# Products within chunks of two heads, and rates of two directions, issued in turn on the two halves of TensorE's rows

## The chip, the cores and the metric

One program runs on one core of a Trainium2 chip. The metric is the device time of one execution in microseconds (us); the median of several executions stands for a kernel.

## What is computed

Two transformer layers of one kind, then one of another kind, on 512 tokens of width 1024, everything in fp32. The change lies in the third layer, in a recurrent branch that the reference writes as a scan over tokens, for 16 heads of 64 and two directions:

```python
def rwkv_prepare(z, shift_w, w0, w_up, a0, a_up, k_k, k_a):
    ...
    w_log = -jax.nn.softplus(-(w0[:, None, None, :] + jnp.einsum('btr,drc->dbtc', jnp.tanh(wd), w_up))) - 0.5
    decay = jnp.exp(-jnp.exp(w_log.astype(jnp.float32)))
    a = jax.nn.sigmoid(a0[:, None, None, :] + jnp.einsum('btr,drc->dbtc', ad, a_up))
    kk = head_l2norm(k * k_k)
    k_eff = k[None] * (1 + (a - 1) * k_a)
    ...

def wkv_scan(s0, scan_in):
    def step(s, inp):
        w, kk, a, k, v, r = inp
        sa = jnp.einsum('dbhij,dbhj->dbhi', s, kk)
        s = s * w[..., None, :] - sa[..., :, None] * (kk * a)[..., None, :] + v[..., :, None] * k[..., None, :]
        return s, jnp.einsum('dbhij,dbhj->dbhi', s, r)
    return lax.scan(step, s0, scan_in)
```

The rates are `a`, from `ad` (64 channels) and `a_up` of each direction. The scan runs over 256 context tokens and then 512 tokens.

## The kernel before, in words

The scan is done in chunks of 64 tokens. Two heads lie side by side on the 128 partitions (0 to 63 and 64 to 127), so there are 8 blocks of channels (`ct`), and each is cut into 3 groups of 4 chunks for each direction (`j` = 0, 1, 2; `j` = 0 is the context): 24 groups in all. A group goes through four pieces of work, each a Python generator:

- `decays` makes the decays and the rates of the group and from them the scaled operands `BK` and `KR`. The rates are two matmuls, one for each direction `d`, of `par[64:128, 2 + d]` with `AD[64:128]`, a contraction over 64 partitions, both on the upper half of TensorE's rows, into the two halves of one PSUM bank.
- `products` multiplies `BK` with `KR` within the chunks, for each direction and each of the two heads `h`: four matmuls contract over the 64 partitions of the head (`H[h]`), write 128 partitions of one bank, and VectorE masks that bank into `G` (line 1702). Then four transposes give `KB`. For `j` = 0 the moving operand has 64 columns, otherwise 128.
- `newton` inverts the triangular parts of `G` of both directions, in 18 steps of fp16 matmuls of 64 x 64 (tile `n`), with ScalarE and VectorE between them.
- `chain` carries the state through the group's 4 chunks, in 13 steps: `X` from state and `VS` (tile `c`), copied to `Xs`, times `U`, copied to `VS` (line 1792), times `KB` to the new state. At its end, for `j` > 0, 16 matmuls of 64 x 64 in fp32 make `O` from `G` and `VS`, and two adds (line 1817) take `O` out of its bank.

The order on each engine is the order of the code (`Pinned`). `weave` runs one slot for each group, of `TT` = 36 ticks: in slot s the chain of group s, the inversions of group s + 1, decays and products of group s + 2, and 48 steps of `fill`, matmuls of 128 rows (tile `mm`) that prepare later blocks. Each piece has a first tick, a last tick and a number of steps that are spread evenly: with `P0` = 17 the six steps of `products` come in ticks 17, 20, 23, 26, 29 and 32; the chain's last step, which makes `O`, comes in tick 27. An fp32 matmul stands in the trace as two weight loads and two matmuls. `xt()` hands out the two banks of tag `x` in turn; rates, products, transposes and `O` all take theirs from it.

Of the kernel before, what the change touches and what calls it, by code (L numbers as in the profile page):

```python
# [10 lines left out]
F32 = mybir.dt.float32  # L11
# [10 lines left out]
T = 512  # L22
NT = T // P
KD = D // P
RWT = 36, 30, 16, 17, 30, 48, 30
FR, SR = 8, 300
FR0 = 2.5, 4
FR1 = 1, 13
# [180 lines left out]
class Net:  # L209
# [1291 lines left out]
    def rwkv(self, hxh, hxl, hch, hcl, mmt2, bank2, lead):  # L1501
# [11 lines left out]
        with ExitStack() as st:  # L1513
# [54 lines left out]
            def block(ct, o):  # L1568

                cs = slice(ct * P, (ct + 1) * P)  # L1570
                o["cs"], o["ct"] = cs, ct
                par = o["par"] = pp.tile([P, 4, P], F32, tag="par", name=self.uid("par"), bufs=2)
                for d in range(2):
                    nc.sync.dma_start(par[0:64, d], a["rw_w_up_2"][0, d, :, cs])
                    nc.sync.dma_start(par[64:65, d], a["rw_w0_2"][0, d:d + 1, cs])
                    nc.sync.dma_start(par[64:128, 2 + d], a["rw_a_up_2"][0, d, :, cs])
                k = o["k"] = tl([P, TA], "k", 2)
                yield from proj(8 + ct, k)

                kks = tl([P, TA], "kks")  # L1580
                nc.vector.tensor_scalar(kks, k, self.kk_[:, ct:ct + 1], None, op0=ALU.mult)
                sq = tl([P, TA], "sq")
                nc.scalar.activation(sq, kks, AF.Square)
                r = o["r"] = tl([P, T], "r", 2)
                yield from proj(ct, r, False)
                ps = xt()
                for t in range(NM):
                    pe.matmul(ps[:, 2 * t:2 * t + 2], sq[:, t * P:(t + 1) * P], c["heads"], start=True, stop=True)
                rn = self.small.tile([P, 2 * NM], F32, tag="rn", name=self.uid("rn"))
                self.rstd(rn, ps[:, :2 * NM], 1.0, 1e-12)  # L1590
                rb = tl([P, TA], "sq").rearrange("p (t h i) -> p t h i", h=2, i=64)
                nc.vector.tensor_copy(rb, rn.rearrange("p (t h) -> p t h", h=2)[:, :, :, None].to_broadcast([P, NM, 2, 64]))
                v = tl([P, TA], "v")
                yield from proj(16 + ct, v)
                kkn = o["kkn"] = tl([P, TA], "kkn", 2)
                for s in rng:
                    ps = xt()
                    n = s.stop - s.start
                    for t in range(n // P):
                        pe.transpose(ps[:, t * P:(t + 1) * P], rb[:, s.start // P + t].rearrange("p h i -> p (h i)"), c["ident"])  # L1600
                    nc.vector.scalar_tensor_tensor(kkn[:, s], ps[:, :n], -0.5, kks[:, s], op0=ALU.mult, op1=ALU.mult)
                    yield
                o["v"] = v
# [27 lines left out]
            def decays(o, g):  # L1631

                ct, j, par = o["ct"], g["j"], o["par"]
                E, Em, ta, ke = tl([P, 2, 4, 65], "E"), tl([P, 2, 4, 64], "Em"), tl([P, 2, C], "ta"), tl([P, 2, C], "ke")
                WC = g["WC"] = tl([P, 2, 4], "WC", 3)
                tok = [slice(P * m0, P * m0 + C) for m0 in pairs(j)]
                ps = xt()
                for d in range(2):
                    for t in range(2):
                        n = tok[d].start + t * P  # L1640
                        pe.matmul(ps[:, (2 * d + t) * P:(2 * d + t + 1) * P], WD[:, n:n + P], par[:65, d], start=True, stop=True)
                th = tl([P, T], "th")
                nc.scalar.activation(th, ps, AF.Tanh, scale=0.5)
                nc.vector.tensor_scalar(th, th, 1.0, None, op0=ALU.add)
                yield
                ps = xt()
                for d in range(2):
                    pe.matmul(ps[:, C * d:C * d + C], par[64:128, 2 + d], AD[64:128, tok[d]], start=True, stop=True)
                for d in range(2):
                    nc.scalar.activation(ta[:, d], ps[:, C * d:C * d + C], AF.Tanh, scale=0.5, bias=self.a0h[:, KD * d + ct:KD * d + ct + 1])  # L1650
                nc.scalar.activation(ke, ta, AF.Identity, scale=self.kah[:, ct:ct + 1], bias=self.kab[:, ct:ct + 1])
                yield
                yield
                ps = xt()
                for d in range(2):
                    for t in range(2):
                        n = (2 * d + t) * P
                        pe.matmul(ps[:, n:n + P], th[:, n:n + P], c["chunk_" + "fb"[d]], start=True, stop=True)
                for d in range(2):
                    o1 = 1 - d  # L1660
                    nc.gpsimd.memset(E[:, d, :, 64 * d:64 * d + 1], 1.0)
                    nc.scalar.activation(E[:, d, :, o1:o1 + 64], ch(ps[:, C * d:C * d + C]), AF.Exp, scale=-K)
                    nc.vector.tensor_copy(WC[:, d], E[:, d, :, 64 * o1])
                nc.scalar.activation(Em.rearrange("p d c s -> p (d c s)"), ps, AF.Exp, scale=K)
                yield

                BK = g["BK"] = tl([P, 2, 2, 4, 64], "BK")
                KR = g["KR"] = tl([P, 2, 2, 4, 64], "KR", 3)
                pr = lambda x: x.rearrange("p (m e) s -> p m e s", e=2)
                for d in range(2):  # L1670
                    o1 = 1 - d
                    nc.gpsimd.tensor_tensor(ke[:, d], ke[:, d], o["k"][:, tok[d]], op=ALU.mult)
                    nc.vector.scalar_tensor_tensor(ta[:, d], ta[:, d], 1.0, o["kkn"][:, tok[d]], op0=ALU.add, op1=ALU.mult)
                    nc.vector.scalar_tensor_tensor(KR[:, d, :, 1:3], pr(ch(o["kkn"][:, tok[d]])), -2.0, pr(E[:, d, :, d:d + 64]), op0=ALU.mult, op1=ALU.mult)
                    if j:
                        xc = slice(tok[d].start - C, tok[d].stop - C)
                        nc.gpsimd.tensor_tensor(KR[:, d, :, 0:4:3], pr(ch(o["r"][:, xc])), pr(E[:, d, :, o1:o1 + 64]), op=ALU.mult)
                    nc.vector.tensor_tensor(BK[:, d, :, 1:3], pr(ch(ta[:, d])), pr(Em[:, d]), op=ALU.mult)
                    nc.vector.tensor_tensor(BK[:, d, :, 0:4:3], pr(ch(ke[:, d])), pr(Em[:, d]), op=ALU.mult)
                    yield  # L1680

            def products(o, g):
# [5 lines left out]
                for d in range(2):  # L1688
                    G = tl([P, 2, 4, P], "G", 5)
                    g["G"].append(G)  # L1690
                    for h in range(2):
                        rows = H[h]
                        ps = xt()
                        for i in range(4):
                            e = i % 2
                            if j:
                                pe.matmul(ps[:, P * i:P * i + P], bk2(rows, d, i),
                                          KR[rows, d, i // 2, 2 * e:2 * e + 2].rearrange("p a s -> p (a s)"), start=True, stop=True)
                            else:
                                off = P * i + 64 * (1 - e)  # L1700
                                pe.matmul(ps[:, off:off + 64], bk2(rows, d, i), KR[rows, d, i // 2, 1 + e], start=True, stop=True)
                        nc.vector.tensor_tensor(G[:, h].rearrange("p (m e) n -> p m (e n)", e=2)[:, :, kc],
                                                ps.rearrange("p (m n) -> p m n", m=2)[:, :, kc],
                                                c["mask_" + "fb"[d]][:, None, kc].to_broadcast([P, 2, kc.stop - kc.start]), op=ALU.mult)
                        yield

                    KB = tl([P, 2, 2, P], "KB", 5)
                    g["KB"].append(KB)
# [111 lines left out]
            def first():  # L1820
                z = tl([P, TA], "v")
                yield from proj(24, z)
                nc.scalar.activation(WD[0:64], z[0:64], AF.Tanh)
                nc.vector.tensor_copy(AD[64:128], z[64:128])
                z = tl([P, TA], "sq")[:, :T]
                yield from proj(25, z, False)
                nc.scalar.activation(SG, z, AF.Tanh, scale=0.5)
                nc.vector.tensor_scalar(SG, SG, 0.5, 0.5, op0=ALU.mult, op1=ALU.add)
# [97 lines left out]
            for s in range(-2, NG_):  # L1926
# [7 lines left out]
                if 0 <= s + 2 < NG_:  # L1934
                    if s > -2:
                        work.append((decays(os_[(s + 2) // 3], gs[s + 2]), 0, DE, 6))
                    work.append((products(os_[(s + 2) // 3], gs[s + 2]), P0, TT, 6))
                if s >= 3 and s % 3 == 0:
                    work.append((self.rwkv_post(os_[s // 3 - 1], tl, xt, SG, pp, pe), 0, TT, 4))
                if s % 3 == 1 and s + 2 < NG_:  # L1940
# [713 lines left out]
```

## Time and profile before

| | us |
|---|---|
| median of 3 runs | 4516.03 (4514.3 to 4528.95) |
| the profiled execution, its own time | 4530.77 |
| its span, first to last instruction | 4529.0 |
| stage of the slots | about 2000 to 3030 |

In the profile PE is TensorE's matmuls, PEld its weight loads, DVE VectorE, ACT ScalarE, POOL GpSimd. Matmuls are pipelined and their ends are modelled, so what a burst of them costs is read from its start to the start of what follows it on the same engine.

### The profile page before, as it was taken

What the parts mean: (1) busy time and instruction counts of PE and PEld (TensorE: products, weight loads), DVE (VectorE), ACT (ScalarE), POOL (GpSimd) and SP (SyncE); (2) the same over time, 40 slices, a digit from 0 to 9 for tenths busy, and PEclk for the clock granted to TensorE, in tenths of its full rate; (3) what the DMA queues carried; (4) which work ended last, traced back from release to release, by engine and by line L of the source; (5) the groups of instructions that cost most, each with busy time, mean ns of one, the idle gap of its engine ahead of it and who ended that gap; (6) DMA issues with size and microseconds to landing.
All of it is one profiled execution on the core that took longest, in us unless ns stands there. A gap on an engine that the chain in (4) does not pass through costs nothing. (4 is left out here: it accounts for less than half of the span.)

```text
span 4529.0 us, 83380 instructions
## 1 busy us (share of the span) xinstructions
PE 4225.4 (93%) x32239; PEld 3671.5 (81%) x32239; DVE 3076.7 (68%) x5903; ACT 1976.1 (44%) x4240; POOL 1698.9 (38%) x1501
## 2 busy tenths in 40 slices
PE   8999999899999899889999999998967889999998
PEld 6889988788888788777777777776866779999997
DVE  4665224656565656555666666645999797999999
ACT  3554234445332545444544455533334444444443
POOL 3324444333443534222333333314465102445443
PEclk8999999899999999989999899999989999999999
DMA  4325334333555422100000001156237557999997
GB/s 136 80 72 148 95 98 125 84 80 112 160 188 183 126 56 59 44 27 22 25 26 26 25 27 35 47 165 215 90 117 223 190 163 260 341 341 343 333 339 261
DMA packets 436982, 620.88 MB, mean 137 GB/s; under 512 B 32852, under 2 KB 318692, under 8 KB 436456
## 3 DMA queue, kind: packets, MB, share of 16 engines
q1 hardware_dynamic: 393384, 471.97, 33.3%
q0 software_dynamic: 36864, 134.23, 8.3%
q10 hardware_dynamic: 6336, 9.35, 0.7%
q8 instruction: 253, 4.15, 0.4%
q14 instruction: 145, 1.19, 0.1%
HBM read 549.36 MB, written 48.24 MB: 132 GB/s over the span
## 5 line engine op out<-in xcount | busy, mean ns | idle before, releaser
L62 POOL TENSOR_TENSOR wlo<-wraw,whi 128x512 fp32r<-128x512 f32 x451 | 613.1, 1365 | 887.9 <-ACT whi L62 849.1
L62 ACT CAST whi<-wraw 128x512 fp32r<-128x512 f32 x572 | 347.5, 617 | 556.3 <-PE mm L62 360.2
L62 PE MATMUL acc<-v,ah 128*128 128x512 f32 x1536 | 419.7, 396 | 4.3 <-ACT ah L62 4.3
L62 PE MATMUL u<-hph,u 128*128 128x384 f32 x1504 | 398.8, 336 | 0.0
L62 PE MATMUL mm<-whi,u 128*128 128x256 f32 x2048 | 377.8, 285 | 4.1 <-ACT u L62 2.4
L1497 POOL TENSOR_TENSOR wbl<-wblk,wbh 128x256 fp32r<-128x256 f32 (+1 forms) x184 | 149.9, 815 | 568.3 <-ACT wbh L1496 363.6
L62 PE MATMUL mm<-xh,whi 128*128 128x512 f32 (+2 forms) x880 | 342.7, 389 | 8.1 <-ACT r L62 5.1
L62 PEld LDWEIGHTS acc<-v,ah 128*128 128x128 f32 x1536 | 292.5, 191 | 60.3 <-ACT ah L62 4.6
L62 PE MATMUL mm<-xl,whi 128*128 128x512 f32 (+2 forms) x880 | 329.1, 374 | 0.0
L62 PEld LDWEIGHTS mm<-whi,u 128*128 128x128 f32 x2048 | 323.9, 194 | 6.1 <-ACT u L62 3.0
L62 PE MATMUL mm<-xh,wlo 128*128 128x512 f32 (+2 forms) x880 | 328.9, 374 | 0.0
L62 PE MATMUL mm<-wlo,u 128*128 128x256 f32 x1024 | 291.8, 285 | 4.9 <-POOL wlo L62 4.6
L62 PEld LDWEIGHTS u<-hph,u 128*128 128x128 f32 x1504 | 273.1, 188 | 3.7
L62 PE MATMUL acc<-v,al 128*128 128x512 f32 x768 | 243.8, 399 | 25.9 <-DVE al L62 25.9
L2555 POOL DMA_INDIRECT gr<-in_peer_u_dram,ei x128 | 165.0, 1289 | 251.7 <-DVE act L2569 158.3
L62 PE MATMUL u<-hpl,u 128*128 128x384 f32 x752 | 252.7, 336 | 0.0
L2555 POOL DMA_INDIRECT gr<-in_peer_v_dram,ei x128 | 170.0, 1328 | 183.4 <-DVE pr L2576 152.8
L62 PE MATMUL mm<-whi,xh 128*128 128x256 f32 x768 | 237.2, 309 | 0.0
L62 PE MATMUL mm<-whi,xl 128*128 128x256 f32 x768 | 220.8, 287 | 1.0 <-POOL xl L62 1.0
L62 PE MATMUL mm<-wlo,xh 128*128 128x256 f32 x768 | 220.3, 287 | 0.0
L62 PEld LDWEIGHTS mm<-wlo,u 128*128 128x128 f32 x1024 | 198.2, 194 | 6.2 <-POOL wlo L62 5.4
L62 DVE TENSOR_TENSOR wlo<-wraw,whi 128x512 fp32r<-128x512 f32 x121 | 102.5, 847 | 147.8 <-ACT whi L62 141.8
(598 smaller groups left out, 11876.2 us busy)
## 6 DMA issues: line engine op xcount, KB each, us to landing
raw<-in_ut_dram SPq DMA_DIRECT2D x128, 512.0 KB
raw<-in_peer_v_dram SPq DMA_DIRECT2D x128, 512.0 KB
wraw<-in_w_in_dram SPq DMA_DIRECT2D x184, 256.0 KB
wraw<-in_w_down_dram SPq DMA_DIRECT2D x160, 256.0 KB
wraw<-in_w_up_dram SPq DMA_DIRECT2D x152, 256.0 KB
mraw<-in_w_mod_dram SPq DMA_DIRECT2D x96, 256.0 KB
wg<-stage SPq DMA_DIRECT2D x12, 2048.0 KB
W<-wg SPq DMA_DIRECT2D x32, 768.0 KB
```

The source lines that it names most:

```text
L62: return lambda *a, **k: self.tc.keep_in_program_order(f(*a, **k))
L1497: (nc.vector if self.wn > WN and n % 2 else nc.gpsimd).tensor_tensor(lo, raw, hi.bitcast(F32), op=ALU.subtract)
L2555: tc.keep_in_program_order(nc.gpsimd.indirect_dma_start(out=r, out_offset=None, in_=w, in_offset=bass.IndirectOffsetOnAxis(ap=ei[:, i:i + ...
```

## The change

The four products of one head are no longer issued in one step and those of the other in the next. Both heads get a bank each at once, and the matmuls go head 0, head 1, head 0, head 1, and so on; both masks follow, and one yield. `products` then has four steps, which with `P0` = 20 come in ticks 20, 24, 28 and 32. The rates get one half of the rows for each direction, and a bank each: `par` and `AD` hold them on both halves, for which one DMA copies 64 x 768 values of `AD` once.

```diff
-RWT = 36, 30, 16, 17, 30, 48, 30
+RWT = 36, 30, 16, 20, 30, 48, 30
...
-                par = o["par"] = pp.tile([P, 4, P], F32, tag="par", name=self.uid("par"), bufs=2)
+                par = o["par"] = pp.tile([P, 3, P], F32, tag="par", name=self.uid("par"), bufs=2)
...
-                    nc.sync.dma_start(par[64:128, 2 + d], a["rw_a_up_2"][0, d, :, cs])
+                    nc.sync.dma_start(par[H[d], 2], a["rw_a_up_2"][0, d, :, cs])
...
-                ps = xt()
+                pss = [xt()[:, :C], xt()[:, :C]]
                 for d in range(2):
-                    pe.matmul(ps[:, C * d:C * d + C], par[64:128, 2 + d], AD[64:128, tok[d]], start=True, stop=True)
+                    pe.matmul(pss[d], par[H[d], 2], AD[H[d], tok[d]], start=True, stop=True)
                 for d in range(2):
-                    nc.scalar.activation(ta[:, d], ps[:, C * d:C * d + C], AF.Tanh, scale=0.5, bias=self.a0h[:, KD * d + ct:KD * d + ct + 1])
+                    nc.scalar.activation(ta[:, d], pss[d], AF.Tanh, scale=0.5, bias=self.a0h[:, KD * d + ct:KD * d + ct + 1])
...
-                    for h in range(2):
-                        rows = H[h]
-                        ps = xt()
-                        for i in range(4):
-                            e = i % 2
+
+                    pss = [xt(), xt()]
+                    for i in range(4):
+                        e = i % 2
+                        for rows, ps in zip(H, pss):
                             if j:
                                 pe.matmul(ps[:, P * i:P * i + P], bk2(rows, d, i),
                                           KR[rows, d, i // 2, 2 * e:2 * e + 2].rearrange("p a s -> p (a s)"), start=True, stop=True)
                             else:
                                 off = P * i + 64 * (1 - e)
                                 pe.matmul(ps[:, off:off + 64], bk2(rows, d, i), KR[rows, d, i // 2, 1 + e], start=True, stop=True)
+                    for h, ps in enumerate(pss):
                         nc.vector.tensor_tensor(G[:, h].rearrange("p (m e) n -> p m (e n)", e=2)[:, :, kc],
...
-                        yield
+                    yield
...
+                nc.sync.dma_start(AD[0:64], z[64:128])
...
-                    work.append((products(os_[(s + 2) // 3], gs[s + 2]), P0, TT, 6))
+                    work.append((products(os_[(s + 2) // 3], gs[s + 2]), P0, TT, 4))
```

**First direction, TensorE, before**, in the slot from 2480 us on: the first head's products (tick 17) stand between an inversion step with one `fill` matmul and the chain's `KB` step; the second head's come in tick 20.

```order
L62 MATMUL n_5506_29434<-Ai_5503_29414,Zi_5487_29324 64x64
L62 MATMUL mm_29178<-xh_15464,wbh_29258 128x512
L62 MATMUL x_29453<-KR_29327,BK_29326 128x128 x4
L62 MATMUL mm_29178<-xl_15465,wbh_29258 128x512
L62 MATMUL c_20467<-VS_29002,KB_28133 64x64 x2
L62 MATMUL c_20467<-VS_29002,KB_28315 64x64 x2
```

**The same products after**: both heads' stand where the second head's stood, after the inversion step on `N`; the banks are `x_29534` (head 0) and `x_29535` (head 1).

```order
L62 MATMUL n_5533_29522<-Yi_5521_29458,N_20471 64x64
L62 MATMUL x_29534<-KR_29342,BK_29341 128x128
L62 MATMUL x_29535<-KR_29342,BK_29341 128x128
L62 MATMUL x_29534<-KR_29342,BK_29341 128x128
L62 MATMUL x_29535<-KR_29342,BK_29341 128x128
L62 MATMUL x_29534<-KR_29342,BK_29341 128x128
L62 MATMUL x_29535<-KR_29342,BK_29341 128x128
L62 MATMUL x_29534<-KR_29342,BK_29341 128x128
L62 MATMUL x_29535<-KR_29342,BK_29341 128x128
L62 MATMUL mm_29193<-xh_15464,wbl_29274 128x512
```

The burst of tick 17 is gone from before the chain's `KB` step; one alternating burst stands in tick 20.

**Second direction, TensorE, before**: the first head's products stand right ahead of the chain's `O` (`x<-VS,G`), and the second head's three ticks later.

```order
L62 MATMUL n_5544_29625<-Yi_5535_29574,N_20469 64x64
L62 MATMUL x_29637<-KR_29327,BK_29326 128x128 x4
L62 MATMUL mm_29544<-xl_15465,wbh_29367 128x512
L62 MATMUL x_29644<-VS_29002,G_27998 64x64 x2
L62 MATMUL x_29644<-VS_29002,G_28201 64x64 x2
```

**The second direction's products after**: they stand behind the inversion step that follows `O`, in the tick after it.

```order
L62 MATMUL n_5563_29684<-Ai_5559_29649,Zi_5553_29617 64x64
L62 MATMUL x_29696<-KR_29342,BK_29341 128x128
L62 MATMUL x_29697<-KR_29342,BK_29341 128x128
L62 MATMUL x_29696<-KR_29342,BK_29341 128x128
L62 MATMUL x_29697<-KR_29342,BK_29341 128x128
L62 MATMUL x_29696<-KR_29342,BK_29341 128x128
L62 MATMUL x_29697<-KR_29342,BK_29341 128x128
L62 MATMUL x_29696<-KR_29342,BK_29341 128x128
L62 MATMUL x_29697<-KR_29342,BK_29341 128x128
L62 MATMUL mm_29560<-hcl,wbh_29382 128x256
```

Nothing of the products now stands ahead of `O`; `O` takes one of the two banks just before the burst that needs both.

## Rows read from the trace of the kernel before

**Rows 1.** Page, part 1: busy time, share of the span, instructions

```profile
PE 4225.4 (93%) x32239; PEld 3671.5 (81%) x32239; DVE 3076.7 (68%) x5903; ACT 1976.1 (44%) x4240; POOL 1698.9 (38%) x1501
```

**Rows 2.** Stretches: length, busy of PE, PEld, DVE, ACT, POOL; clock, DMA

```profile
2000.00:3000.00 1000.00, 964.64 (x12446) 760.00 (x12447) 629.20 (x1576) 486.58 (x1377) 317.25 (x475) 0.96 0.12 37
2400.00:2550.00 150.00, 144.97 (x1835) 114.52 (x1833) 97.46 (x240) 70.43 (x199) 54.46 (x77) 0.91 0.09 25
2700.00:2850.00 150.00, 147.72 (x1939) 117.07 (x1939) 93.65 (x243) 78.18 (x228) 49.90 (x76) 1.00 0.11 34
```

**Rows 3.** Waits of PE, 2000 to 3000: total us, times, longest (first, last)

```profile
PE c L62 <- DVE S L1804: 8.0, 9, 1.3
...
PE x L62 <- ACT KB L1712: 0.2, 1, 0.2
```

**Rows 4.** Instructions of the products: ns min/median/max, first and last start

```profile
L62 PEld LDWEIGHTS x<-KR,BK x768: 182/188/189, 1998.8 to 2935.9; 64*128 64x128 f32 x192
L62 PE MATMUL x<-KR,BK x768: 272/272/374, 1998.8 to 2936.0; 64*128 64x128 f32 x128, 64*128 64x64 f32 x64
```

**Rows 5.** Timeline around a tick 17: start us, us, instruction

```profile
2509.83 0.63 PE L62 MATMUL c<-Xs,U 128*128 128x64 f32 x4 [0.41 <-DVE Y L1782]
...
2510.79 0.28 DVE L1792 COPY VS<-c 64x128 f32<-64x128 f32 x1 [1.10 <-ACT VS L1792]
...
2511.19 0.96 PEld L62 LDWEIGHTS x<-KR,BK 64*128 64x128 f32 x8 [0.25 <-issue]
2511.19 1.16 PE L62 MATMUL x<-KR,BK 64*128 64x128 f32 x8
...
2512.28 0.49 PE L62 MATMUL mm<-xl,wbh 128*128 128x512 f32 x1
2512.38 0.69 DVE L1702 TENSOR_TENSOR G<-x,tables 128x512 f32<-128x512 f32 x1 [1.31 <-PE x L62]
2512.70 0.39 PE L62 MATMUL c<-VS,KB 128*64 128x64 f32 x6
```

**Rows 6.** Timeline, a burst of `j` = 0 (64 moving columns) and what follows

```profile
2220.38 1.10 PE L62 MATMUL x<-KR,BK 64*128 64x64 f32 x8
2221.41 0.49 PE L62 MATMUL mm<-xl,wbh 128*128 128x512 f32 x1
```

**Rows 7.** Timeline, one `O`: loads and matmuls

```profile
2655.20 1.18 PEld L62 LDWEIGHTS x<-VS,G 64*64 64x64 f32 x32
2655.20 1.32 PE L62 MATMUL x<-VS,G 64*64 64x64 f32 x32
```

**Rows 8.** Weight loads of `O`: ns min/median/max, first and last start

```profile
L62 PEld LDWEIGHTS x<-VS,G x512: 129/135/136, 2109.0 to 3031.0; 64*64 64x64 f32 x171
```

**Rows 9.** Timeline, one burst of the rates and what follows

```profile
2577.36 1.13 PE L62 MATMUL x<-AD,par 64*128 64x256 f32 x4
2578.42 0.50 PE L62 MATMUL mm<-xh,wbl 128*128 128x512 f32 x1
```

**Rows 10.** Timeline, second direction's products and `O` in one slot

```profile
2521.11 0.75 DVE L1990 SCALAR_TENSOR_TENSOR Ai<-tables,n 128x256 f16<-128x256 f32 x2 [0.58 <-PE n L62]
2521.14 1.16 PE L62 MATMUL x<-KR,BK 64*128 64x128 f32 x8
...
2522.66 1.32 PE L62 MATMUL x<-VS,G 64*64 64x64 f32 x32
...
2523.96 0.69 DVE L1702 TENSOR_TENSOR G<-x,tables 128x512 f32<-128x512 f32 x1 [0.58 <-PE x L62]
...
2524.46 0.44 PE L62 MATMUL n<-Ai,Zi 64*64 64x64 f16 x16
2524.57 0.74 DVE L1817 TENSOR_TENSOR Y<-Y,x 128x256 f32<-128x256 f32 x2
...
2525.14 1.16 PE L62 MATMUL x<-KR,BK 64*128 64x128 f32 x8
```

**Rows 11.** Masks into `G` on DVE: ns min/median/max, first and last start

```profile
L1702 DVE TENSOR_TENSOR G<-x,tables x96: 423/690/693, 2000.2 to 2936.3; 128x512 f32<-128x512 f32 x64, 128x256 f32<-128x256 f32 x32
```

## The prediction

> **What bounds the kernel now.** I read the page first: TensorE's matmuls are busy for 93% of the span, and no other engine passes 68% [rows 1]. That share is a mean over stages, so next come the stretches of the stage in which the change lies. From 2000 to 3000 us PE is busy for 964.64 of 1000 us, its weight loads for 760, VectorE for 629, ScalarE for 487, GpSimd for 317, and the DMA engines for 12% [rows 2]. Then PE's waits in that stage: ten rows, of which the first and the last stand in [rows 3], add up to 35 us. So in this stage TensorE is nearly always at work, the others are not, and what it no longer has to do should come off the time. Behind the stage the program goes on with work that needs its results, so an earlier end is passed on.
>
> How much does it have to do for the products? The group has 768 matmuls and 768 loads [rows 4], which is 96 bursts of 8: 24 groups, 2 directions, 2 heads, and four fp32 products each in two passes. One burst lasts from 2511.19 to 2512.28, where the next matmul starts: 1.09 us [rows 5]. With half as many moving columns it lasts from 2220.38 to 2221.41: 1.03 us [rows 6]. Halving the columns takes only 0.06 us off, so it is not the moving operand that sets the pace but the loading of the 128 stationary columns: 8 loads in 0.96 us, the last of them 0.19 long [rows 4, 5], are (0.96 - 0.19) / 7 = 0.11 us apart. The other 0.21 us of a burst (1.09 - 8 x 0.11) go into entering and leaving it. 64 bursts of 1.09 and 32 of 1.03 are 103 us of the stage.
>
> **The change part by part.**
>
> Products. The question is whether the loads and matmuls of two halves of the rows go on side by side. The trace has fp32 bursts in which both halves are used: `O`, whose 16 matmuls go to one half and the other in runs of two and four. Its 32 loads, each 0.135 us [rows 8], start within 1.18 - 0.135 us, so 0.034 us apart [rows 7]. In a row, at half of the 0.11 us above for half the columns, they would be 0.055 apart (an estimate). They overlap, then, and take 0.61 of the serial time; 0.50 would be perfect. In `O` the halves also differ in the output partitions, while the products of both heads write the same 128 partitions of two banks; no row here shows that, and it is the first thing that can fail. By `O`'s ratio the 16 loads of a direction take 16 x 0.11 x 0.61 = 1.08 us, and with 0.21 the burst is 1.29; perfect overlap gives 0.88 + 0.21 = 1.09. Before, a direction takes 2 x 1.09 = 2.18 us (2.06 for `j` = 0). It saves 0.89 to 1.09 us (0.77 to 0.97 for `j` = 0), and over 32 and 16 directions 41 to 50 us. The strict alternation suits overlap better than `O`'s runs, but `O`'s halves share nothing; I take the middle, 46.
>
> The Trainium skill has a figure for this ("TensorE: Matmul & The Clock Gate", section "Measured speedup vs the span model"): four row tiles gave 3.07 times, not four. At that efficiency two halves would give 1.53 times, an estimate, the burst would be 16 x 0.11 / 1.53 + 0.21 = 1.36 us, and the products would save 37 us. The overlap in `O` is better than this.
>
> Rates. One burst lasts from 2577.36 to 2578.42, 1.06 us [rows 9]: four passes of 256 columns, (1.06 - 0.21) / 4 = 0.21 each. With one direction on each half, two steps instead of four: 0.42 us saved, or 0.33 at `O`'s ratio. 24 of them: 8 to 10 us; I take 9. The extra DMA is one, once, in front of the stage; it costs the queue of SP a wait for `z`, with weight blocks queued behind it that are loaded ahead of use. I set it at nothing; if that cover fails, it is paid once and not in each slot.
>
> Masks. Their number and size stay the same (0.69 us, 96 of them, [rows 11]), but the two of a direction now come in a row, 1.38 us of VectorE. Nothing needs the second one soon: the `KB` step is four ticks later, some 4.5 us (about 25 slots of 36 ticks lie between 2000 and 3030 us).
>
> Where the stall goes. A burst that is taken away shortens what lies between a result and its use. In tick 17 the chain's `KB` step needs the copies to `VS`, which end at 2510.79 + 0.28 = 2511.07; it starts at 2512.70 [rows 5]. That is 1.63 us of slack, and 1.09 us are taken: it holds. In the second direction the burst at 2521.14 lies between an inversion step and the next, whose `Ai` is ready at 2521.11 + 0.75 = 2521.86 and used at 2524.46 [rows 10]: 2.6 us of slack, it holds too. Late next is the bank. After the change `O` holds one of the two banks that the second direction's burst needs, and that burst follows `O` by two `fill` matmuls and one inversion step. Now the adds that free `O`'s bank run from 2524.57 to 2525.31, behind a mask of 0.69 us [rows 10]; PE would arrive when the inversion step ends, at 2524.46 + 0.44 = 2524.90. If the adds stay as late, each of the 16 slots with an `O` waits 0.41 us, 7 us in all; but the mask ahead of them moves behind the burst, and without it they end 0.7 earlier. I take half, 4 us. `chain` and `newton` are queued behind a PE that waits there, so each such wait delays the slot. Of the rest I let a tenth come back as waits elsewhere, 5 us: I could not follow every pair of result and use.
>
> **The sum**: 46 + 9 - 4 - 5 = 46 us. The profiled execution took 4530.77 us and would become 4485; it lies 14.7 us above the median of the runs, 4516.03, which becomes **4470**. Terms at their ends: 50 + 10 = 60 and no loss, 4456; 41 + 8 - 7 - 10 = 32, 4484. What the granted clock adds: the stretch at 0.91 issued 1835 matmuls, that at 1.00 1939 [rows 2], 5.4% fewer for 0.09. A change of 0.01 to 0.02 in the stage's mean of 0.96 is 6 to 12 us either way. That makes 4446 to 4495 the likeliest case's own range.
>
> **The rivals.**
>
> *No overlap where the outputs are the same partitions.* Then 16 loads stay 0.11 us apart: 1.76 + 0.21 = 1.97 us against 2.18 or 2.06, which saves 32 x 0.21 + 16 x 0.09 = 8 us (one entry fewer); the rates save nothing, and the wait for the bank takes 4: 4512, no change. For it: no row shows this form. Against it: the loads set the pace, and in `O` loads of two halves do go on together. Chance 0.10.
>
> *VectorE takes the time back.* If the second mask of each pair stands in front of a copy that the chain waits for, 0.69 us are lost in each of 48 bursts, 33 us: 46 - 33 = 13 saved, 4503; with half of them hit, 4487. For it: VectorE is busy 63% of the stage [rows 2] and works its queue in order. Against it: the order puts the masks behind the chain's copies of the same tick, and PE waits for all engines together only 35 us in 1000 [rows 3]. It decides once a copy of the chain stands behind a pair of masks in each burst. Chance 0.15, about 4495 as its middle. The Trainium skill speaks for this one ("TensorEngine Tiling (Array Packing)", section "PSUM Bottleneck"): tiling speeds up TensorE but not the emptying of PSUM, so the copies may become the bound. The trace has VectorE at two thirds, which is not yet that.
>
> *Slower: each change of half costs an exposed load.* The first matmul of a burst takes up to 0.374 us, against 0.272 for the others [rows 4]: 0.10 for a load that nothing hides. If seven changes of half in each burst cost that, without overlap, it is 1.97 + 0.7 = 2.67 us, 0.49 more than now (0.61 for `j` = 0), 25 us; with 0.10 for each of 24 bursts of rates and 4 for the bank, 4516 + 32 = 4548. It decides where a change of half costs over (2.18 - 1.97) / 7 = 0.03 us. Against it: `O` changes halves four times and still loads faster than in a row [rows 7]. Chance 0.07.
>
> **How the numbers follow.** The forecast has 0.68. A measurement of this kernel can tell about 0.3%, 13.5 us, from no change. Faster by more: the forecast, and nearly all of VectorE's case: 0.82. Within: no overlap, and the end of VectorE's case: 0.11. Slower: 0.07. The range runs from 4446 to 4506; it takes in VectorE's case and leaves out no overlap and the slower one, 0.17 together, and a little of the low end.
>
> **What would show it.** Bursts of 16 in the products of 1.1 to 1.3 us; if they are near 2.0, the halves do not overlap, and above 2.2 changing halves costs. Rates of 0.6 to 0.75 us. The wait of PE for the adds of `O` or for `G`'s mask: under 10 us together, or VectorE's case is true. PE's waits of the stage should stay under 55 us, and the stage should end about 46 us earlier in the profile. The sum is wrong above all if the granted clock of the stage moves by more than 0.02, or if a wait that now hides behind the burst of tick 17 appears in all slots.

## The result and the profile after

The changed kernel takes 4451.32 us (median of 4 runs, 4448.15 to 4456.57), the kernel before 4515.16 (4 runs, 4513.12 to 4528.95) in the same comparison: the ratio is 0.9856, 95% interval 0.9836 to 0.9876. That is 64 us faster, where 46 were forecast. The profiled execution took 4451.97 us, its span is 4450.2 us and its mean granted clock 0.966 (before: 0.961).

The page, part 1, of the changed kernel, beside [rows 1]:

```profile
PE 4139.1 (93%) x32239; PEld 3601.2 (81%) x32239; DVE 3076.5 (69%) x5903; ACT 1979.0 (44%) x4240; POOL 1698.1 (38%) x1501
```

The instructions are the same in number, matmuls and loads alike. Their busy time is 86 us less on PE; VectorE has the same work in a shorter span. The last matmuls of the last `O` start at 2955 us, before at 3031 [rows 8]: the stage ends 76 us earlier (the two profiled executions are 79 us apart, the medians 64). The stretches of the stage, beside [rows 2] (length, busy time of PE, PEld, DVE, ACT, POOL, granted clock, DMA):

```profile
2000.00:2950.00 950.00, 906.38 (x12573) 711.63 (x12572) 633.58 (x1595) 494.88 (x1392) 320.98 (x472) 0.97 0.14 43
2400.00:2550.00 150.00, 141.11 (x1954) 111.83 (x1954) 100.38 (x257) 79.05 (x224) 50.20 (x75) 0.97 0.09 26
2700.00:2850.00 150.00, 145.78 (x2075) 111.42 (x2074) 100.52 (x252) 81.30 (x233) 68.71 (x98) 1.00 0.16 48
```

950 us now hold slightly more instructions of PE than 1000 did. PE is still busy for 95% of them: TensorE has less to do and remains the bound. The timeline of PE at a burst of `j` = 0 (2203.14), then of all engines at one of `j` > 0 (2520.72), then of PE at the rates (2758.42), beside [rows 5, 6, 9]:

```profile
2203.14 1.11 PE L62 MATMUL x<-KR,BK 64*128 64x64 f32 x16
2204.18 0.39 PE L62 MATMUL mm<-hch,wbl 128*128 128x256 f32 x1
...
2520.72 0.97 PEld L62 LDWEIGHTS x<-KR,BK 64*128 64x128 f32 x16
2520.72 1.16 PE L62 MATMUL x<-KR,BK 64*128 64x128 f32 x16
...
2521.81 0.19 PEld L62 LDWEIGHTS mm<-xl,wbh 128*128 128x128 f32 x1
2521.81 0.50 PE L62 MATMUL mm<-xl,wbh 128*128 128x512 f32 x1
2521.91 1.29 DVE L1703 TENSOR_TENSOR G<-x,tables 128x512 f32<-128x512 f32 x2
...
2758.42 0.70 PE L62 MATMUL x<-AD,par 64*128 64x256 f32 x4
2759.06 0.50 PE L62 MATMUL mm<-xl,wbh 128*128 128x512 f32 x1
```

Read each from its start to the start of what follows. Sixteen loads and matmuls of both heads take 2521.81 - 2520.72 = 1.09 us, which is what eight of one head took before: the sixteen loads are done in 0.97 us, where eight took 0.96 [rows 5]. With 64 moving columns it is 1.04 us. The rates take 0.64 us, before 1.06. The 48 bursts of the products sum to 53.5 us, the 96 of before to 102.5: 49 us less. The 24 of the rates save 10.

PE's waits from 1990 to 3000 us (total us, times, longest); those of [rows 3] begin at 2000:

```profile
PE c L62 <- DVE VS L1793: 7.6, 12, 1.4
PE c L62 <- DVE S L1805: 6.9, 9, 2.2
PE n L62 <- ACT Zi L1985: 6.1, 7, 1.2
...
PE x L62 <- DVE G L1703: 1.0, 2, 0.6
...
PE c L62 <- DVE Xs L1776: 0.2, 1, 0.2
```

All fourteen rows sum to 44 us, against 38 of the kernel before in the same stretch. The wait for a bank that a mask still reads (`x <- DVE G`) is 1.0 us, and it is transposes of `BK` that wait there. No wait for the adds of `O` stands in the list. Of the 48 bursts of the products one waits, the second, for the bank that `kkn` still reads:

```profile
2017.58 1.16 PE L62 MATMUL x<-KR,BK 64*128 64x128 f32 x14 [0.64 <-DVE kkn L1601]
```

**A finer measure than the whole time.** Executions of one kernel differ by 10 us and more, much of it with the granted clock. A slot whose clock was 1.00 throughout has no such difference. The transposes of `BK` open each slot, so the start of the first of them and that of the last of the next slot's first four, in one row, give a slot's length plus 0.4 us. Here is the sixth slot, at clock 1.00 in each kernel (duration min/median/max, first and last start): before, after, and the changed kernel run again as a control.

```profile
L62 PE MATMUL x<-tables,BK x12: 272/273/328, 2187.4 to 2228.2; 128*128 128x128 f32 x12
```

```profile
L62 PE MATMUL x<-tables,BK x12: 272/273/328, 2169.3 to 2207.1; 128*128 128x128 f32 x12
```

```profile
L63 PE MATMUL x<-tables,BK x12: 272/273/328, 2168.6 to 2206.4; 128*128 128x128 f32 x12
```

40.8 us before, 37.8 after, and 37.8 again. Over the slots that have clock 1.00 in both traces of a pair, the control's differ from those of the changed kernel by 0.01 us in the median (15 slots); those of the changed kernel are 2.47 us shorter than before's in the median and 2.45 in the mean (14 slots). If the other slots shortened alike, 24 of 2.45 us are 59 us.

### The profile page after: what moved, and what is told of

Same layout as the page of the kernel before. It is cut to its first block, busy times and chain, and to the rows that moved or that the text cites. A ratio compares the mean times of both kernels' runs of the same rounds, so it can differ in the third digit from the quotient of the medians.

```text
span 4450.2 us, 83415 instructions
## 1 busy us (share of the span) xinstructions
PE 4139.1 (93%) x32239; PEld 3601.2 (81%) x32239; DVE 3076.5 (69%) x5903; ACT 1979.0 (44%) x4240; POOL 1698.1 (38%) x1501
## 3 DMA queue, kind: packets, MB, share of 16 engines
q14 instruction: 145, 1.19, 0.1%
## 5 line engine op out<-in xcount | busy, mean ns | idle before, releaser
L62 DVE TENSOR_TENSOR wlo<-wraw,whi 128x512 fp32r<-128x512 f32 x121 | 102.5, 847 | 147.2 <-ACT whi L62 141.5
```

The lines of the kernel that those rows point to most:

```text
L62: return lambda *a, **k: self.tc.keep_in_program_order(f(*a, **k))
```

## The experiments

Ratios are to the kernel before, run on the same chip. None of these kernels leaves out a part of the computation; some do a part several times with the same values.

**The two parts alone.** In `products_only` the rates stay as they were:

```diff
-                pss = [xt()[:, :C], xt()[:, :C]]
+                ps = xt()
...
-                    pe.matmul(pss[d], par[H[d], 2], AD[H[d], tok[d]], start=True, stop=True)
+                    pe.matmul(ps[:, C * d:C * d + C], par[64:128, 2 + d], AD[64:128, tok[d]], start=True, stop=True)
```

> The changed kernel with the rates as they were before (both directions on the upper half, one bank). Theory A, the two parts add up and PE sets the pace of the stage: 24 bursts of rates cost 0.42 us more again, 10 us, so about 4461 us against 4451 of the changed kernel, and the bursts of products stay at 1.09 us. Rival B, the rates lie in the slack of the chain and gave nothing: 4451 us.

Measured: 4463.23 us (6 runs), ratio 0.9866 (0.9846 to 0.9887), 60 us faster. Its bursts are 1.09 us for the products and 1.06 for the rates. Nearly all of the gain is the products'.

`rates_only` is the kernel before with the other part, the rates and their DMA, and the products untouched.

> The kernel before with the new rates alone. Theory A: 10 us less than before, about 4505 us, rates of 0.63 us. Rival B: they lie in slack, 4515 us, no change. If the two parts together give more than the sum of each alone, a wait is shared by both.

Measured: 4518.09 us (12 runs), ratio 0.9996 (0.9980 to 1.0012): between 9 us faster and 5 slower, so the 10 us of TensorE are not seen in the time; up to 9 of them can be there. The sixth slot of the two, `products_only` first:

```profile
L62 PE MATMUL x<-tables,BK x12: 272/272/328, 2171.4 to 2209.6; 128*128 128x128 f32 x12
```

```profile
L62 PE MATMUL x<-tables,BK x12: 272/273/327, 2187.3 to 2227.7; 128*128 128x128 f32 x12
```

The products take 2.6 us off this slot (40.8 to 38.2), the rates alone 0.4 (to 40.4), and the rates on top of the products again 0.4 (38.2 to 37.8). Over all slots at clock 1.00 the medians are 2.27 (14 slots), 0.42 (12) and 0.41 (15). In the slots the 0.42 us of the burst are there, in the whole time they are not seen (the mean of the 12 slots of `rates_only` is 0.31, 7 us over 24, which its interval allows). To tell apart whether the place of the rates has slack or the clock hides them, the changed kernel was run with the rates four times over:

```diff
-                for d in range(2):
+                for d in (0, 1) * 4:
                     pe.matmul(pss[d], par[H[d], 2], AD[H[d], tok[d]], start=True, stop=True)
```

> The changed kernel with each of the two rate matmuls issued four times into its bank, in turn (the same values each time). A burst of rates should grow from 0.633 us by six further steps of 0.21 us to about 1.9 us; 24 of them add about 30 us to TensorE. It asks why the rates alone, done in the kernel before, gave nothing that could be measured, although their bursts are 10 us shorter. Theory A, what TensorE has to do in the rates goes into the time as it does in the products, and the missing 10 us of the rates alone were lost in the spread of the granted clock: about 30 us slower than the changed kernel, near 4482, ratio 0.992 to kernel before (0.990 to 0.994). Rival B, the place of the rates has slack behind it (the decays that follow wait for ScalarE and VectorE and the slot's end is set elsewhere), so that their length matters little: under 12 us slower, below 4464, ratio up to 0.988. The granted clock can move either by 10 us; the length of a slot in the trace at full clock (37.6 us now) decides with it: 38.9 by A, under 38.1 by B.

Measured: 4473.78 us (6 runs), ratio 0.9897 (0.9875 to 0.9919). The control's ratio in its own comparison was 0.9853, so it is some 20 us slower, between the two expectations; the slot decides. One burst of the rates on PE, and the sixth slot:

```profile
2734.00 2.00 PE L63 MATMUL x<-AD,par 64*128 64x256 f32 x16
2735.92 0.50 PE L63 MATMUL mm<-xl,wbh 128*128 128x512 f32 x1
```

```profile
L63 PE MATMUL x<-tables,BK x12: 272/273/328, 2171.9 to 2211.0; 128*128 128x128 f32 x12
```

The burst takes 1.92 us, 1.28 more, and the slot 39.1 us, 1.3 more; the median over 17 slots is 1.31. So there is no slack behind the rates: what they take goes into the slot in full (theory A). Its stage had a granted clock of 0.99 from 2000 to 2950 us, against 0.97 in the changed kernel and 0.96 in the control, which may be where the rest of the 30 us went; one profile cannot show that.

**How the halves overlap.** `one_step_no_turns` keeps both heads in one step with two banks, but issues four products of one head and then four of the other:

```diff
-                    for i in range(4):
-                        e = i % 2
-                        for rows, ps in zip(H, pss):
+                    for rows, ps in zip(H, pss):
+                        for i in range(4):
+                            e = i % 2
```

> The changed kernel, two banks and the same ticks, but all four products of head 0 and then all four of head 1. Theory A, overlap needs the turns, since eight loads of one half stand ahead of the other half's first: bursts of 16 x 0.11 + 0.21 = 1.97 us, 48 x 0.88 = 42 us more than the changed kernel, 4493 us. Rival B, PE starts the second half's loads over the head of the first half's, as the runs of four in O suggest: bursts of 1.1 to 1.3 us and 4451 to 4460 us. Rival C, the time came from the other ticks and the fewer steps and not from overlap: bursts near 2 us and still about 4451 us.

Measured: 4469.08 us (6 runs), ratio 0.9876 (0.9856 to 0.9897). PE at one burst, then at one of `turns_of_two`, which changes the head after two products:

```diff
+                    for m, rows, ps, e in [(m, rows, ps, e) for m in range(2) for rows, ps in zip(H, pss) for e in range(2)]:
+                        for i in (2 * m + e,):
```

> The changed kernel with turns of two products (four loads) instead of one. With all four in a row the bursts took 1.64 us, 13 steps of 0.11 and 0.21: PE began the second half's loads when three of the first half's eight were left. Theory A, PE looks about three loads ahead: runs of four loads then cost one step more than strict turns, bursts of about 1.2 us, and 5 us more than the changed kernel. Rival B, only loads next to each other overlap: bursts of 1.4 us or more, 15 us more.

```profile
2482.07 1.71 PE L62 MATMUL x<-KR,BK 64*128 64x128 f32 x16
2483.71 0.50 PE L62 MATMUL mm<-xh,wbl 128*128 128x512 f32 x1
```

```profile
2488.90 1.26 PE L62 MATMUL x<-KR,BK 64*128 64x128 f32 x16
2490.09 0.50 PE L62 MATMUL mm<-xh,wbl 128*128 128x512 f32 x1
```

1.64 us without turns, 1.19 with turns of two products, 1.09 with turns of one. At 0.11 us for a load and 0.21 for entering and leaving, that is 13, 9 and 8 steps for the same 16 loads. The first was expected by none of the theories (1.97 or 1.1 to 1.3): when the second head's eight loads follow the first head's, only about three of them go beside the first's. The longer bursts show in the slots: without turns 1.04 us more in the median (16 slots), for two bursts that are 0.55 longer each; turns of two 0.16 (15 slots), for two that are 0.10 longer. `turns_of_two` took 4457.02 us (5 runs), ratio 0.9862 (0.9827 to 0.9897), not to be told from the changed kernel.

`tick_22_o_turns` brings the turns to `O` as well (two matmuls in a row on one half stand only where one step of four meets the next), and moves the first tick of the products from 20 to 22:

```diff
-RWT = 36, 30, 16, 20, 30, 48, 30
+RWT = 36, 30, 16, 22, 30, 48, 30
...
-                        for d, i in enumerate((s, 3 - s)):
-                            e, n = i % 2, C * d + P * (i // 2)
-                            for h in range(2):
+                        for h in range(2):
+                            for d, i in enumerate((s, 3 - s)):
+                                e, n = i % 2, C * d + P * (i // 2)
```

> The changed kernel with the first tick of the products at 22 and the matmuls of O in strict turns of the halves. Theory A, the second direction's burst stands further behind O, whose bank it needs, and O itself shrinks from 1.25 to about 1.1 us in 16 slots: 3 to 6 us less than the changed kernel. Rival B, masks and KB come too late for the next slot's inversion: 10 us or more on top.

```profile
2488.29 1.15 PE L62 MATMUL x<-VS,G 64*64 64x64 f32 x32
2489.37 0.50 PE L62 MATMUL mm<-xh,wbl 128*128 128x512 f32 x1
```

`O` takes 1.08 us, where before and after the change it takes 1.25: here too a shorter run on one half overlaps more. The time did not follow: 4465.49 us (6 runs), ratio 0.9876 (0.9842 to 0.9910), and slots 0.58 us longer in the median (14). Two things were moved at once, and which of them cost that was not tried. It is no wait that the profile names: PE's waits sum to 42 us, where the control's sum to 44, and the wait for `N`, behind the masks, is 0.6 us, that for `KB` 0.2.

**How much of TensorE's work reaches the time.** `products_twice` issues all products of the changed kernel twice:

```diff
-                    for i in range(4):
+                    for i in (0, 1, 2, 3) * 2:
```

> The changed kernel with each alternating burst of products issued twice over (the second writes the same values again). PE has 8 more steps of 0.11 us in each of 48 bursts, 42 us. Theory A, PE sets the pace of the stage, so that all of it comes on top: about 0.9395 of a per cent, ratio near 0.995 of the kernel before. Rival B, what PE saves or spends here falls half into waits: ratio near 0.990.

```profile
2496.45 2.06 PE L62 MATMUL x<-KR,BK 64*128 64x128 f32 x32
2498.44 0.50 PE L62 MATMUL mm<-xh,wbl 128*128 128x512 f32 x1
```

```profile
L62 PE MATMUL x<-tables,BK x12: 272/273/328, 2175.1 to 2214.7; 128*128 128x128 f32 x12
```

Bursts of 1.99 us, 0.90 more, 43 us over all 48; the slot is 39.6 us, 1.8 more for its two bursts, and the median of 13 slots is 1.79 too (mean 2.01). The whole time is 4514.29 us (12 runs), ratio 0.9986 (0.9968 to 1.0004), 60 us above the control's: more than the 43, at a mean clock of 0.962 against 0.965. In the slots the added work arrives whole; that the rest of the 60 is the clock is argued from these two means, not shown.

`changed_again`, the control of that comparison, is the changed kernel itself.

> The changed kernel itself, on the chip of the next three, so that they can be held against it: 0.9856 of the kernel before, as measured first.

Measured: 4452.23 us (5 runs), ratio 0.9853 (0.9838 to 0.9869), PE's waits 44 us.

`before_tick_20` is the kernel before with the fourth value of `RWT` at 20 and nothing else:

> The kernel before with nothing changed but the first tick of the products, 20 instead of 17; its six steps stay apart. Theory A, the change gave what PE's bursts became shorter by and the ticks gave nothing: bursts stay at 1.03 and 1.09 us and the time is that of before within 0.3%. Rival B, the shorter bursts explain 50 of some 60 us and the other ticks the rest: 0.2 to 0.4% faster than before with the same bursts.

Measured: 4513.22 us (12 runs), ratio 0.9992 (0.9981 to 1.0003), bursts as before, slots 0.10 us longer in the median (10), single ones from 0.8 shorter to 0.7 longer. The new ticks alone give nothing that can be told from noise.

**The banks.** `first_tick_18` is the changed kernel with that value at 18, which puts the second direction's products right behind `O`:

```diff
-RWT = 36, 30, 16, 20, 30, 48, 30
+RWT = 36, 30, 16, 18, 30, 48, 30
```

> The changed kernel with the first tick of the products at 18 instead of 20, which puts the second direction's burst right behind O, whose bank it needs. Theory A, the wait for the bank is real but hidden in the changed kernel by the two fill matmuls and the inversion step between: now PE waits for the adds of O, 0.6 to 1.3 us in each of 16 slots, 10 to 20 us more, about 4466 us. Rival B, the order of these steps does not matter because PE has enough queued: 4451 us.

Measured: 4501.01 us (9 runs), ratio 0.9948 (0.9928 to 0.9969), some 40 us slower than the changed kernel. PE's waits of the stage, and the timeline at one `O`:

```profile
PE n L62 <- ACT Yi L1985: 9.1, 9, 1.4
PE x L62 <- DVE Y L1818: 8.8, 14, 1.6
PE x L62 <- DVE G L1703: 8.1, 8, 1.4
```

```profile
2499.72 1.32 PE L62 MATMUL x<-VS,G 64*64 64x64 f32 x32
2500.96 0.48 PE L62 MATMUL x<-KR,BK 64*128 64x128 f32 x2
...
2502.20 0.75 DVE L1818 TENSOR_TENSOR Y<-Y,x 128x256 f32<-128x256 f32 x2
2503.06 0.96 PEld L62 LDWEIGHTS x<-KR,BK 64*128 64x128 f32 x14 [1.81 <-issue]
2503.09 1.13 PE L62 MATMUL x<-KR,BK 64*128 64x128 f32 x14 [1.65 <-DVE Y L1818]
```

Head 0's first product (two passes) goes to the free bank; head 1's needs the bank of `O`, and PE stands still for 1.65 us until the adds have emptied it. Of the three rows of waits the first is a late inversion step; the other two, 17 us together, are banks: the products wait for the adds of `O`, the transposes for masks. By start to start the bursts of the products sum to 75 us in this execution, 22 more than in the changed kernel. What the other half of the 40 us is was not tried; 10 to 20 us were expected.

**VectorE.** `masks_twice` does every pair of masks twice:

```diff
-                    for h, ps in enumerate(pss):
+                    for h, ps in (*enumerate(pss), *enumerate(pss)):
```

> The changed kernel with each mask of a pair done twice (same values): 48 x 1.38 = 66 us more of VectorE, up to 2.8 us in a row. Theory A, VectorE has room and its queue is not on the path: under 0.2% more than the changed kernel. Rival B, the emptying of PSUM is nearly the bound and the chain's copies stand behind the masks: 33 us or more, 0.7%.

Measured: 4483.84 us (6 runs), ratio 0.9923 (0.9906 to 0.9939), 31 us above the control for 96 more masks. By their durations these are 57 us and not the 66 that were expected: 64 masks take 0.69 us, but the 32 of `j` = 0 take 0.42 [rows 11]. The first row of PE's waits, and the stage:

```profile
PE n L62 <- DVE N L1737: 11.5, 8, 1.7
```

```profile
2000.00:2950.00 950.00, 893.48 (x12310) 700.03 (x12310) 662.55 (x1654) 486.61 (x1369) 315.95 (x468) 0.95 0.13 37
```

A new wait stands first: the inversion waits for `N`, a VectorE operation behind the masks. Slots at clock 1.00 are 0.39 us longer in the median and 0.54 in the mean (11 slots), 9 to 13 us over 24; the rest of the 31 goes with a lower clock, 0.95 in this stage (the control's 0.96) and 0.961 in the mean of the runs (0.965).

`less_on_vector` goes the other way and gives two small operations of VectorE in each slot to GpSimd:

```diff
-                nc.vector.tensor_scalar(th, th, 1.0, None, op0=ALU.add)
+                nc.gpsimd.tensor_scalar(th, th, 1.0, None, op0=ALU.add)
...
-                    nc.vector.tensor_copy(VS[64:128, d, :, 1], o["V"][64:128, m0:m0 + 2])
+                    nc.gpsimd.tensor_copy(VS[64:128, d, :, 1], o["V"][64:128, m0:m0 + 2])
```

> The changed kernel with two steps of VectorE put on GpSimd (24 additions of 0.43 us to th, 48 copies of 0.3 to 0.4 us to VS): 28 us less in VectorE's queue. Theory A, since 66 us more of masks cost about 30 us, VectorE's queue is partly on the path: 7 to 13 us less than the changed kernel. Rival B, doubled masks only hurt by standing in a row, or GpSimd delays the weights: no gain.

Measured: 4463.71 us (6 runs), ratio 0.9883 (0.9852 to 0.9915). Its page, part 1, one row of PE's waits, and a stretch behind one such wait:

```profile
PE 4147.8 (93%) x32239; PEld 3608.1 (81%) x32239; DVE 3048.9 (68%) x5831; ACT 1978.8 (44%) x4240; POOL 1753.6 (39%) x1573
```

```profile
PE x L62 <- POOL th L1644: 7.3, 4, 2.2
```

```profile
2149.00:2152.40 3.40, 3.28 (x14) 3.18 (x15) 0.74 (x2) 0.66 (x2) 2.83 (x6) 0.51 0.06 14
```

VectorE is busy for 28 us less (3048.9 against 3076.5), and the slots have the same length in the median (0.00, 12 slots; 0.24 us longer in the mean). But the addition takes 1.50 us on GpSimd, where VectorE took 0.43, and PE now waits for it in four slots, 7.3 us in all. In three of these, whose clock was 1.00 in the changed kernel, TensorE stood still for 1.6 to 2.2 us, and at the end of that wait or within 2 us of it the granted clock fell to 0.5, the lower of its two levels (1.2 GHz), for 3.4 us. So the whole time, by the ratios some 12 us above the changed kernel's, cannot tell what VectorE is worth. The slots without such a wait can: except for one, 0.4 us shorter, they do not become shorter by more than 0.1 us with less work on VectorE, so no limit by VectorE is seen in them.

## Why the prediction held, step by step

The direction, the place of the gain and its mechanism were right. The gain was 64 us instead of 46: three terms were off, all in the same direction. 4451 is even below 4456, the sum with every term at its best end; it lies in the likeliest case's own range only because of what was added there for the granted clock. That it fell inside is in part luck. By terms:

- **What bounds**: shown. `products_twice` and `rates_four_times` add work to TensorE alone, and the slots grow by 1.8 us for 1.8 and by 1.3 for 1.3.
- **Products, 46 us**: measured 49, next to the perfect end of the bounds (50). The halves overlap in full, although the heads write the same 128 partitions of two banks; this was the first thing that could fail, and it did not. The middle was chosen because `O` overlaps only to 0.61 of the serial time and its halves "share nothing". That was read wrongly: what `O` lacks are turns. Its runs of two and four on one half cost it, as runs do in `one_step_no_turns` (13 steps of load instead of 8), and with turns `O` itself came down from 1.25 to 1.08 us.
- **The Trainium skill's figure**: 3.07 for four row tiles ("TensorE: Matmul & The Clock Gate", section "Measured speedup vs the span model") would have given a burst of 1.36 us, an estimate. The trace has 1.09; the measurement decides, for two halves of fp32 in strict turn.
- **Rates, 9 us**: the bursts gave 10, and each slot at clock 1.00 is 0.4 us shorter for them. In the whole time of `rates_only` at most 9 of the 10 us can have been there.
- **The wait for the bank, 4 us**: mis-sized; for the adds of `O` none was measured, for other holders of a bank 1.6 us (1.0 and 0.6). The step itself (`O` holds one of two banks) was right, and `first_tick_18` shows its price where the burst stands closer behind `O`: 1.65 us in one slot, 8.8 us in the stage.
- **A tenth back as waits, 5 us**: mis-sized. PE's waits grew from 38 to 44 us, but the slots became shorter by 2.45 us in the mean, 59 us in all, which is 49 + 10: nothing came back.
- **Granted clock, 6 to 12 us either way**: of the 64 us, 59 are slots; 5 are left, which fits a mean clock that was 0.965 in the control's runs and 0.964 in those of the kernel before beside it. That these 5 are the clock is argued, not shown; the interval of the ratio, 56 to 74 us, allows 59 as well.
- **VectorE takes the time back**: it did not in this kernel; the slots became shorter by all that TensorE's bursts gave. The price of this rival was also set too high: a third of the masks take 0.42 us and not 0.69. The Trainium skill's rule ("TensorEngine Tiling (Array Packing)", section "PSUM Bottleneck") points at a limit that is near all the same: with the masks doubled, the slots grow by 0.39 to 0.54 us and PE waits first of all for VectorE.
- **No overlap, and an exposed load at each change of half**: both fell with the burst of 1.09 us; seven changes of half within a burst cost nothing that can be seen.

Open: how much of the rates alone reaches the time of the whole kernel (the interval allows 9 us), what the second half of the loss in `first_tick_18` is, and what made the slots of `tick_22_o_turns` longer.

## What to carry to other kernels

Where weight loads set the pace and the contraction takes 64 rows, issue the products of two halves strictly in turn, into a bank for each: two bursts then cost one, even if both write the same partitions, and longer runs on one half lose part of it. Before placing such a burst, see who holds the banks: it takes two at once, and two ticks nearer to another holder took back 40 of 64 us, about half of it in the bursts that wait. Work that is moved to another engine can make TensorE wait there instead, as the addition on GpSimd did. When the clock blurs the whole time, compare single slots at full clock: in two executions of one kernel they repeat to 0.01 us. Take many of them, since in another order of the same work single slots differ by up to 0.8 us (`before_tick_20`).

## What the hardware showed beyond expectation

- TensorE's loads on two halves of the rows overlap by how they are ordered: 16 loads take 8, 9 or 13 steps of 0.11 us in turns of one product, two products, and none.
- A kernel's slots at clock 1.00 repeat to 0.01 us in the median between two executions, while whole executions of the control went from 4446.41 to 4460.81 us.
- 57 us more of work on VectorE cost 31 us of time, of which the slots at clock 1.00 account for only 9 to 13; the granted clock of the stage was 0.95, the control's 0.96. How a wait can cost more than its length is seen in `less_on_vector`: three waits of 1.6 to 2.2 us for GpSimd were each followed by 3.4 us at the lower level of TensorE's clock. Whether that is the cause in `masks_twice` was not tried.
